# One layer with RWKV-7 and HGRN2 branches: the whole body in one block ordered by a timeline simulation

## The chip, the cores and the metric

The kernel runs on one core of a Trainium2 chip. Its engines are TensorE (PE, matmuls and transposes), VectorE (DVE), ScalarE (ACT), GpSimdE (POOL) and SyncE (SP, which issues DMAs here). Each engine has its own queue of instructions, and the queues meet only at semaphores. The metric is the time of one execution on the device in microseconds (us), the median of several runs; a profile shows one execution.

## The reference, cut to what matters

One layer is applied to a prompt of 512 tokens and to 8 sequences of 4 new tokens each, with their own states. Everything is float32.

```
h   = rmsnorm(x) * norm_mix_g
u   = h @ w_in                       # [tokens, 1024] @ [1024, 5888]
u_a, u_b, u_g = split(u)             # 2048 | 1792 | 2048 columns
o_a = hgrn2(u_a)                     # 4 heads of 128: gated linear attention, norm, gate
o_b = rwkv7(mix(u_b, previous u_b))  # 8 heads of 64: delta rule, group norm, bonus, gate
x   = x + (sigmoid(u_ga) * (o_a @ w_a_out) + sigmoid(u_gb) * (o_b @ w_b_out)) @ w_out
x   = x + square(relu(rmsnorm(x) @ w_up)) @ w_down      # 1024 -> 4096 -> 1024
y   = rmsnorm(x) * norm_final_g
```

Results are y, the last row of h, and the final states of both branches.

## The kernel before

Channels lie on the partitions, and the 512 + 32 tokens (with 8 rows of the shift state for u_b) are the columns, in two halves of about 272, each with a PSUM bank. A float32 weight tile is split into a high part (whi, a copy by ACT to a shorter mantissa) and a low part (wlo, the rest, by DVE), and so are the activations; a product is three groups of matmuls: high by high, low by high, high by low (`split`, line 166, `gemm_h`, line 398).

The program is written as one long Python function, `hybrid_step` (line 61). After the norm of the input (`stats`, `transposed`, `normed`, in the order of the string STARTUP) a loop goes through the string ORDER. Each entry multiplies one column tile of w_in (`in_unit`, line 410: 48 matmuls of 128 x 128 by 128 x 272 or so) and takes it to its place: `b_unit` for RWKV inputs, `a_unit` for HGRN2 inputs, `gate_unit` for the gates. There are 46 such tiles. Between them two background lanes are advanced by a fixed number of steps (`pump`, line 1270); each is a list of Python generators, and a `yield` ends a step.

- Lane X runs `rw_all(0)`, `rw_all(1)` (line 977) and then `hg_head` 3. An `rw_all` prepares two head pairs (`rw_batch`), inverts and solves small triangular blocks (`rw_inverse`, `rw_solve`), carries the state through eight chunks (`rw_chain`, line 760) and normalises the output of each pair (`gn` and `rw_out`, lines 819 and 834). In a step of `rw_chain` each operation needs the one before: pq from the state (PE), ch (DVE), pq from ch (PE), VU (DVE), pq from VU (PE), the state st (DVE). `gn` is a sum, a subtraction, a square (ACT), a sum, an inverse root in twelve small operations (`rsq`, line 143) and a product; `rw_out` transposes (rw_out_pt), scales (og, ACT), adds, gates, and writes og to ob_d in DRAM.
- Lane Y runs `hg_head` 0 and 1, the sample states (`rw_state`, `rw_sample`, `hg_sample`) and `hg_head` 2. `hg_head` (line 1068) scans the decays (hb), goes through five levels and two more in which DVE writes E, ACT takes its exponential, DVE writes X and PE multiplies (hg_head_pl, hg_head_pu; `decayed`, line 1056), masks and adds the products (sm, ad), transposes, makes the state (hst) and the output (hg_head_po, hy), normalises it (squares jk on ACT, `rsq` on DVE) and writes hog to oa_d in DRAM. In PSUM, lane X has two pools of its own and lane Y another.

When ORDER is done the rest of lane X is emitted, then the branch results are read back and merged: `branch(ob_d)` loads ox and splits it into oh (ACT) and ol (DVE); `half_unit` (line 1343) multiplies them by w_b_out, while lane Y is finished; `branch(oa_d)` and w_a_out follow, then `full_unit` (line 1400) for w_out, w_up and w_down. At the end `finish` (line 1455) transposes each channel tile of the result to tokens (fin_t, one PSUM bank), adds up squares and multiplies by the weight; `final` scales and stores.

What sets the order: the framework turns the Python calls into instructions, assigns each to the engine that the call names, and adds the semaphores. A scheduler of its own then puts each engine's instructions in an order; the program gives it the order of the calls and no block of its own. Instructions marked with `tc.keep_in_program_order` (the constants written by POOL, class Late) stay in the order of the calls.

Of the kernel before, what the change touches and what calls it, by code (L numbers as in the profile page):

```python
# [60 lines left out]
def hybrid_step(ctx: ExitStack, tc: tile.TileContext, i, o):  # L61
    nc = tc.nc
# [46 lines left out]
    class Lane:  # L109
        """slots and PSUM banks of one of the two background lanes"""  # L110
# [32 lines left out]
    def rsq(x, scale=None, eps=None):  # L143
        """x <- (x * scale + eps) ** -0.5 of a few columns: a guess from the exponent, three Newton steps"""
        n, m = x.shape
# [28 lines left out]
    def load8(src, c):  # L174
        """columns c..c+128 of a [1024, *] weight as [p, 8, 128]"""
        st = pipe.tile([128, 1024], F32, tag="stage", name=nm("st"), bufs=NST)
        nc.sync.dma_start(out=st.rearrange("p (k c) -> p k c", k=8),
                          in_=src[:, c:c + 128].rearrange("(k p) c -> p k c", p=128))
        return st

# [31 lines left out]
    def stats(t):  # L212
        """1 / rms of every token of a tile, on every partition"""
# [52 lines left out]
    class Late:  # L266
        """Pool operations that stay behind those already queued"""
# [17 lines left out]
    def consts1():  # L285
# [5 lines left out]
        # masks of the RWKV pair products, rows s, columns t: [A_vk^T | A_re^T] over [A_zb^T (negated) | A_rb^T]  # L291
# [8 lines left out]
    def consts2():  # L300
        # masks of the HGRN2 levels inside 32-token blocks: s in the even half, t in the odd half
        late.memset(lmk, 1.0)
        for l, h in enumerate((16, 8, 4, 2, 1)):
            nb = 32 // (2 * h)
            for b in range(4):
                v = lmk[32 * b:32 * b + 32, l, :].rearrange("p (n w) -> p n w", n=nb)
                # t odd half
                late.memset(v[:, :, 0:h], 0.0)
                # s >= 2h*n  and  s < 2h*n + h
# [9 lines left out]
    def consts3():  # L319
        # sample masks: same sequence, strictly causal towards kk, causal towards r  # L320
# [9 lines left out]
        # rows of a sequence: bmk[row, b]  # L330
# [20 lines left out]
    # per-channel parameters, channel on the partition  # L351
# [19 lines left out]
    # sigmoid(x) = (1 + tanh(x / 2)) / 2: halves of the biases, and of the weight behind silu(g)  # L371
# [7 lines left out]
    def load4(src, c):  # L379
        """columns c..c+256 of a [512, *] weight as [p, 4, 256]"""  # L380
# [5 lines left out]
    def gemm(ps, w_hi, w_lo, x_hi, x_lo, n, first=True, last=True, late=0):  # L386
        """lists of [128,128] weight tiles and matching [128, 2n] operands, of which the last few may come late"""
# [10 lines left out]
    def gemm_h(w_hi, w_lo, x_hi, x_lo, cuts, name):  # L398
        """the same products, one bank for each part of the columns"""
# [17 lines left out]
    def b_unit(jt):  # L417
        """column tile jt of the B block -> token-shift mixed [128, 544]"""
# [15 lines left out]
    # low-rank weights: the parts of decay as [hi; lo], of a as [lo; hi], of the gate in two tiles  # L434
# [104 lines left out]
    def head_sums(hi, lo):  # L539
        """sums over the channels of a head, on all of them"""  # L540
# [6 lines left out]
    def rw_batch(pairs, xk, xr, xv):  # L547
        """channel-major preparation and the pair products of two head pairs"""
# [15 lines left out]
        for q, p in enumerate(pairs):  # L564
# [33 lines left out]
            # sample columns: sig, kk, kk*a, k, r, v, bonus  # L598
# [4 lines left out]
            # rows (v side | u side, token), columns (kk | r, token)  # L603
# [22 lines left out]
    def swapped(src, dst):  # L626
        """64x64 transposes within the two halves of the partitions: channels of a head <-> tokens of a chunk"""
# [5 lines left out]
    def rw_values(g):  # L633
        """rows (v | u, token): v, and room for u"""
# [11 lines left out]
    def rw_tokens(p):  # L646
        """A_vk v with rows (head, token); k and b with rows (v | u, token)"""
# [20 lines left out]
    def rw_inverse(g):  # L668
        """(I + A_zb^T)^-1 of the 32x32 diagonal blocks of two pairs.
        16x16 blocks by doubling, one block on a partition (quarter parity, head, half, chunk)"""  # L670
# [39 lines left out]
        # the 32x32 blocks: eight rows of a block on a partition  # L710
# [49 lines left out]
    def rw_chain(g):  # L760
        """the state from chunk to chunk, and the outputs"""
# [850 lines left out]
```

## Time and profile before

| | us |
|---|---|
| median of 3 runs | 1000.02 (999.65 to 1000.9) |
| span of the profiled execution, first to last instruction | 996.1 |
| PE busy | 962.8 |
| DVE busy | 584.3 |
| ACT busy | 394.0 |
| POOL busy | 135.8 |

The profiled execution has no time of its own beside its span; the span lies 3.9 us under the median. A view by stretch gives each engine's busy time between two times, the mean granted clock of PE (1.00 is 2.4 GHz, 0.50 is 1.2 GHz) and the load of the DMA engines. A view in order of time lists an engine's instructions, neighbours that are alike joined in one row with their count; in brackets stands the idle time ahead of a row and what ended it. An instruction's own duration includes its start and its end, and neighbours on one engine overlap by a part of it. Many small matmuls count twice in the trace (8868 there, 7653 in the program).

### The profile page before, as it was taken

How to read it: one execution, taken by the hardware profiler on the slowest of the kernel's cores; microseconds unless marked ns; L12 is line 12 of the kernel's file. 1: busy time of each engine (PE TensorE's matmuls, PEld its weight loads, DVE VectorE, ACT ScalarE, POOL GpSimd, SP SyncE). 2: the span in 40 equal slices, each digit the busy share in tenths (PEclk: the TensorE clock that was granted, in tenths of full speed). 3: DMA queues.
4: the chain of work that ended last, by engine and by line, in shares of the span. 5: the costliest groups of instructions: out<-in, count | busy, mean ns of one | idle time of the engine just before them, and what ended most of it. 6: DMA issues, size and time to landing. Idle time of an engine off the chain costs nothing.

```text
span 996.1 us, 21327 instructions
## 1 busy us (share of the span) xinstructions
PE 962.8 (97%) x8868; PEld 908.1 (91%) x8868; DVE 584.3 (59%) x1198; ACT 394.0 (40%) x722; POOL 135.8 (14%) x328
## 2 busy tenths in 40 slices
PE   5999999999999899999999999999999999999996
PEld 4999988889998886888899999999999999999995
DVE  6635979578696854679878554444222244445333
ACT  7554545514636441334444333333111233333232
POOL 4486423221132101101000000000000000000000
PEclk9999999999999899999999999999999999999998
DMA  9632343222345232445743642322223332234111
GB/s 273 173 105 81 81 91 100 57 66 90 114 107 109 44 107 63 124 135 171 256 122 128 197 128 84 87 85 86 85 86 89 97 90 86 86 106 142 50 44 48
DMA packets 191091, 106.38 MB, mean 107 GB/s; under 512 B 38945, under 2 KB 179047, under 8 KB 190994
## 3 DMA queue, kind: packets, MB, share of 16 engines
q1 hardware_dynamic: 165424, 95.16, 32.8%
q10 hardware_dynamic: 25570, 9.85, 3.9%
q8 instruction: 70, 1.15, 0.5%
q14 instruction: 27, 0.22, 0.1%
HBM read 85.08 MB, written 18.39 MB: 104 GB/s over the span
## 4 chain that ended last, share of the span: by engine, by line
PE 81%; DVE 9%; DMA 4%; ACT 3%; POOL 2%; issue 1%; SPq 1%; ACTq 0%; DVEq 0%; POOLq 0%
PE pd L129 24%; PE in_unit_ps L129 20%; PE full_unit_ps L129 19%; PE half_unit_ps L129 4%; PE rw_chain_pq L129 2%; DVE tmp L135 2%; PE rw_chain_py L129 1%; DVE wlo L135 1%; PE rw_out_pt L129 1%; PE rw_sample_pn L129 1%; PE hg_head_po L129 1%; PE lora_ps L129 1%; DVE bn L724 1%; DMA xin<-in_x_prompt_dram 1%; PE hg_head_pl L129 1%
## 5 line engine op out<-in xcount | busy, mean ns | idle before, releaser
L132 ACT ACTIVATE whi<-st 128x1024 fp32r<-128x1024 f32 x120 | 126.7, 1057 | 251.6 <-PE pd L129 119.2
L135 DVE TENSOR_TENSOR wlo<-st,whi 128x1024 fp32r<-128x1024 f32 x120 | 149.2, 1244 | 126.0 <-PE full_unit_ps L129 40.3
L129 PE MATMUL in_unit_ps<-h_hi,whi 128*128 128x272 f32 (+3 forms) x736 | 121.3, 300 | 2.3 <-ACT h_hi L132 1.4
L129 PE MATMUL in_unit_ps<-h_hi,wlo 128*128 128x272 f32 (+3 forms) x736 | 121.7, 299 | 0.0
L129 PE MATMUL in_unit_ps<-h_lo,whi 128*128 128x272 f32 (+3 forms) x736 | 121.2, 300 | 0.0
L129 PEld LDWEIGHTS in_unit_ps<-h_hi,whi 128*128 128x128 f32 x736 | 103.3, 194 | 8.4 <-issue 3.4
L129 PE MATMUL full_unit_ps<-hd,whi 128*128 128x272 f32 (+2 forms) x832 | 110.3, 289 | 0.0
L129 PEld LDWEIGHTS in_unit_ps<-h_hi,wlo 128*128 128x128 f32 x736 | 103.2, 193 | 4.4 <-issue 2.4
L129 PEld LDWEIGHTS in_unit_ps<-h_lo,whi 128*128 128x128 f32 x736 | 103.7, 194 | 3.8 <-issue 1.9
L129 PEld LDWEIGHTS full_unit_ps<-hd,whi 128*128 128x128 f32 x832 | 106.5, 188 | 0.0
L129 PE MATMUL pd<-xgl,whi 128*128 128x272 f32 x512 | 70.2, 289 | 0.0
L129 PE MATMUL pd<-xgh,wlo 128*128 128x272 f32 x512 | 69.8, 288 | 0.0
L129 PE MATMUL pd<-xgh,whi 128*128 128x272 f32 x512 | 69.8, 288 | 0.0
L141 POOL TENSOR_SCALAR ys<-ys,ssf 32x512 f32<-32x512 f32 x1 | 0.8, 830 | 491.1 <-DVE ssf L1495 491.1
L129 PEld LDWEIGHTS pd<-xgl,whi 128*128 128x128 f32 x512 | 66.7, 188 | 0.0
L129 PEld LDWEIGHTS pd<-xgh,whi 128*128 128x128 f32 x512 | 66.2, 188 | 0.0
L129 PEld LDWEIGHTS pd<-xgh,wlo 128*128 128x128 f32 x512 | 66.2, 188 | 0.0
L129 PE MATMUL full_unit_ps<-hd,wlo 128*128 128x272 f32 (+2 forms) x416 | 56.8, 288 | 0.0
L129 PEld LDWEIGHTS full_unit_ps<-hd,wlo 128*128 128x128 f32 x416 | 54.0, 188 | 0.0
L135 DVE TENSOR_TENSOR hd<-r,hd 128x544 fp32r<-128x544 f32 x32 | 23.2, 725 | 47.9 <-ACT hd L132 47.9
L135 DVE TENSOR_TENSOR x<-x,full_unit_ps 128x272 f32<-128x272 f32 (+2 forms) x48 | 19.5, 434 | 36.9 <-PE full_unit_ps L129 36.9
L138 DVE SCALAR_TENSOR_TENSOR r<-pd,rsb 128x272 f32<-128x272 f32 x64 | 25.2, 435 | 25.9 <-PE pd L129 23.9
(413 smaller groups left out, 1500.9 us busy)
## 6 DMA issues: line engine op xcount, KB each, us to landing
st<-in_w_in_dram SPq DMA_DIRECT2D x46, 512.0 KB
st<-in_w_up_dram SPq DMA_DIRECT2D x32, 512.0 KB
st<-in_w_down_dram SPq DMA_DIRECT2D x32, 512.0 KB
gt_d<-gt SPq DMA_DIRECT2D x16, 272.0 KB
st<-in_w_out_dram SPq DMA_DIRECT2D x8, 512.0 KB
gtb<-gt_d SPq DMA_DIRECT2D x8, 272.0 KB
gta<-gt_d SPq DMA_DIRECT2D x8, 272.0 KB
x<-xt_d SPq DMA_DIRECT2D x8, 272.0 KB
```

What stands on the lines that cost most here:

```text
L129: T.matmul(out, lhsT, rhs, start=start, stop=stop)
L132: A.activation(out=out, in_=in_, func=func, **kw)
L135: (eng or V).tensor_tensor(out=out, in0=a, in1=b, op=op)
L138: V.scalar_tensor_tensor(out=out, in0=a, scalar=s, in1=b, op0=op0, op1=op1)
L141: (eng or V).tensor_scalar(out=out, in0=a, scalar1=s1, scalar2=s2, op0=op0, op1=op1)
L724: V.tensor_reduce(out=o_[:, i0:i1, t0:t1], in_=tp, axis=AX.X, op=ALU.add)
```

## The change

One line is added at the head of `hybrid_step`; the rest of the diff removes comments and docstrings. The line opens a block that lasts to the end of the function, with the option that its instructions are ordered by the scheduler's timeline simulation.

```diff
@@ -59,6 +59,7 @@
 
 @with_exitstack
 def hybrid_step(ctx: ExitStack, tc: tile.TileContext, i, o):
+    ctx.enter_context(tc.block(schedule_with_timeline_sim=True))
     nc = tc.nc
     V, A, P, T = nc.vector, nc.scalar, nc.gpsimd, nc.tensor
     DQ = nc.scalar
@@ -107,7 +108,7 @@
         return psy.tile([128, 512], F32, tag="y", name=nm(name))
 
     class Lane:
-        """slots and PSUM banks of one of the two background lanes"""
+
 
         def __init__(self, S, two, one):
...
         (eng or V).tensor_scalar(out=out, in0=a, scalar1=s1, scalar2=s2, op0=op0, op1=op1)
 
     def rsq(x, scale=None, eps=None):
-        """x <- (x * scale + eps) ** -0.5 of a few columns: a guess from the exponent, three Newton steps"""
+
         n, m = x.shape
         y, t = (small.tile([128, 16], F32, tag=f"rs{e}", name=nm("rs"))[0:n, 0:m] for e in range(2))
         if scale is not None:
...
```

The instructions are the same ones on PE (7653), DVE (1197), POOL (333) and SP (287); ACT has 746 instead of 744, two more loads of its function table. Their order differs on all five engines. In the order after every number behind a tile's name is one higher and every line one further down.

PE, at the place where the products of w_in end and those of w_b_out begin, before (h_hi and h_lo are the normed input; rows that lie between are left out):

```order
L129 MATMUL in_unit_ps_6210<-h_hi,wlo_6207 128x272 x8
L129 MATMUL in_unit_ps_6210<-h_lo,whi_6206 128x272 x8
...
L1159 MATMUL hg_head_pt_5821<-ident,hy_5791 128x128 x4
L1254 MATMUL hg_sample_pt_6017<-ident,hs_5360 128x128
...
L129 MATMUL in_unit_ps_6270<-h_hi,wlo_6267 128x272 x8
...
L129 MATMUL in_unit_ps_6295<-h_hi,wlo_6267 128x272 x8
L129 MATMUL in_unit_ps_6295<-h_lo,whi_6266 128x272 x8
L129 MATMUL hg_head_pl_6326<-X_6331 32x32 x8
L129 MATMUL hg_head_pl_6327<-X_6331 32x32 x8
...
L129 MATMUL half_unit_ps_6423<-oh_6393,whi_6417 128x272
L129 MATMUL half_unit_ps_6436<-oh_6393,whi_6417 128x272
```

The same place after:

```order
L130 MATMUL in_unit_ps_6296<-h_lo,whi_6267 128x272 x8
L130 MATMUL hg_sample_pn_5765<-svm_5763,xt_5540 128x512
L130 MATMUL rw_chain_pq_4894<-st_4708,kr_3680 64x64 x2
...
L130 MATMUL rw_chain_pq_5006<-st_4708,kr_3680 64x64 x2
...
L811 MATMUL rw_chain_pw_5034<-ident,st_4708 64x128
...
L632 MATMUL rw_out_pt_5063<-ident,yo_5030 64x64
...
L130 MATMUL hg_head_pl_5316<-X_5320 32x32 x16
...
L130 MATMUL hg_head_po_5770<-vt_5671,att_5317 128x128 x2
...
L1160 MATMUL hg_head_pt_5822<-ident,hy_5792 128x128 x4
L1255 MATMUL hg_sample_pt_6018<-ident,hs_5361 128x128
L130 MATMUL hg_head_pl_6327<-X_6332 32x32 x8
...
L130 MATMUL half_unit_ps_6424<-oh_6394,whi_6418 128x272
```

Between the last in_unit_ps and the first half_unit_ps stood 33 matmuls, all of hg_head_pl of head 2; now there are 324: three steps of the second chain, its rw_out, head 3 from hg_head_pl to hg_head_pt, the end of hg_sample and the first levels of head 2.

ACT at the same place, before (oa_d<-hog and oa_d<-hs are stores that ACT's queue issues):

```order
L1162 DMA oa_d<-hog_5826 128x512
L132 ACTIVATE gt_6260<-in_unit_ps_6235 128x272
L1258 DMA oa_d<-hs_5361 512x1x32
L132 ACTIVATE E_6376<-E_6376 128x512
L132 ACTIVATE whi_6676<-st_6674 128x1024
L132 ACTIVATE gt_6320<-in_unit_ps_6270 128x272
L132 ACTIVATE E_6468<-E_6468 128x512
L132 ACTIVATE E_6491<-E_6491 128x512
L132 ACTIVATE gt_6320<-in_unit_ps_6295 128x272
L132 ACTIVATE oh_6393<-ox_6391 128x544
```

And after:

```order
L133 ACTIVATE kt_5672<-hg_head_pt_5679 128x512
L133 ACTIVATE hst_5750<-hg_head_pk_5745 128x128
L1142 DMA out_dram<-hst_5750 128x128
L133 ACTIVATE hy_5792<-hg_head_po_5770 128x512
L133 ACTIVATE jk_5794,ss_h<-hy_5792 128x128 x4
L1163 DMA oa_d<-hog_5827 128x512
L1259 DMA oa_d<-hs_5362 512x1x32
L133 ACTIVATE oh_6394<-ox_6392 128x544
L133 ACTIVATE oh_6400<-ox_6398 128x544
```

The first oh now stands behind hy, the squares jk and the two stores; before, exponentials, weight splits and gates of in_units stood between.

PE around the last step of the first RWKV chain (rw_chain_pq_2774 before, rw_chain_pq_2775 after), before:

```order
L129 MATMUL rw_chain_pq_2774<-st_2128,kr_1323 64x64 x2
L129 MATMUL rw_chain_pq_2774<-st_2129,kr_1466 64x64 x2
L129 MATMUL in_unit_ps_3035<-h_lo,whi_3006 128x272 x5
L129 MATMUL in_unit_ps_3171<-h_hi,whi_3167 128x276 x6
L129 MATMUL rw_chain_pq_2774<-ch_2130,TT_1850 64x128
L129 MATMUL rw_chain_pq_2774<-ch_2130,TT_2017 64x128
L129 MATMUL in_unit_ps_3171<-h_hi,whi_3167 128x276 x2
L129 MATMUL in_unit_ps_3171<-h_hi,wlo_3168 128x276 x4
L129 MATMUL rw_chain_pq_2774<-VU_1572,BE_1612 64x64 x2
L129 MATMUL rw_chain_pq_2774<-VU_1572,BE_1652 64x64 x2
L129 MATMUL rw_chain_py_2127<-VU_1572,A_1347 64x64
```

And after, with rows left out:

```order
L130 MATMUL in_unit_ps_4549<-h_lo,whi_4545 128x272 x8
L130 MATMUL rw_chain_pq_2645<-VU_1573,BE_1613 64x64 x2
...
L130 MATMUL rw_chain_pq_2775<-st_2129,kr_1324 64x64 x2
...
L130 MATMUL rw_chain_pq_2775<-ch_2131,TT_1851 64x128
...
L130 MATMUL rw_chain_pq_2775<-VU_1573,BE_1613 64x64 x2
...
L811 MATMUL rw_chain_pw_2825<-ident,st_2129 64x128
...
L632 MATMUL rw_out_pt_2930<-ident,yo_2821 64x64
...
L632 MATMUL rw_out_pt_3095<-ident,yo_2823 64x64
...
L1160 MATMUL hg_head_pt_3495<-ident,hy_3473 128x128 x4
L642 MATMUL rw_batch_pt_4084<-ident,xm_2903 64x128
...
L130 MATMUL in_unit_ps_4574<-h_hi,whi_4545 128x272 x8
```

In_units stood between the parts of the step; now 92 matmuls of the chain's end, of rw_out, of head 1, of the next rw_batch and of rw_state follow each other without one, between two halves of one w_in tile.

## Rows read from the trace of the kernel before

**Rows 1.** The page: busy time of the engines, the chain by engine, one costly group.
```profile
PE 962.8 (97%) x8868; PEld 908.1 (91%) x8868; DVE 584.3 (59%) x1198; ACT 394.0 (40%) x722; POOL 135.8 (14%) x328
...
PE 81%; DVE 9%; DMA 4%; ACT 3%; POOL 2%; issue 1%; SPq 1%; ACTq 0%; DVEq 0%; POOLq 0%
...
L132 ACT ACTIVATE whi<-st 128x1024 fp32r<-128x1024 f32 x120 | 126.7, 1057 | 251.6 <-PE pd L129 119.2
```

**Rows 2.** Busy time by stretch; its columns: stretch, us, engines, PEclk, DMA share, GB/s.
```profile
25.00:485.00 460.00, 449.49 (x4643) 400.58 (x4643) 331.04 (x731) 207.93 (x390) 122.52 (x304) 0.97 0.38 103
485.00:546.00 61.00, 58.78 (x641) 56.07 (x640) 49.18 (x107) 26.01 (x46) 1.53 (x5) 1.00 0.53 171
546.00:985.00 439.00, 439.00 (x3505) 438.68 (x3504) 183.75 (x285) 137.26 (x226) 0.00 (x0) 1.00 0.32 92
```

**Rows 3.** PE in order of time; columns: start us, us, engine, line, operation [idle before].
```profile
484.36 1.17 PE L129 MATMUL in_unit_ps<-h_lo,whi 128*128 128x272 f32 x8
485.45 0.78 PE L129 MATMUL hg_head_pl<-X 128*32 128x32 f32 x66
487.17 0.52 PE L129 MATMUL half_unit_ps<-oh,whi 128*128 128x272 f32 x2 [0.94 <-ACT oh L132]
...
490.42 0.52 PE L129 MATMUL half_unit_ps<-oh,whi 128*128 128x272 f32 x2
```

**Rows 4.** ACT in order of time at the same place.
```profile
486.46 0.66 ACT L132 ACTIVATE oh<-ox 128x544 fp32r<-128x544 f32 x1 [0.51 <-DMA ox<-ob_d]
...
487.98 1.74 ACT L132 ACTIVATE oh<-ox 128x544 fp32r<-128x544 f32 x3
```

**Rows 5.** PE in order of time, one step of the first RWKV chain and the next one's start.
```profile
195.40 0.45 PE L129 MATMUL rw_chain_pq<-st,kr 64*64 64x64 f32 x8
...
199.89 0.45 PE L129 MATMUL rw_chain_pq<-st,kr 64*64 64x64 f32 x8
```

**Rows 6.** DVE in order of time, a norm, its og, an operation of the next one.
```profile
225.21 1.28 DVE L822 TENSOR_REDUCE gs<-yo 128x8 f32<-128x512 f32 x2 [0.65 <-ACT yo L132]
...
235.73 0.68 DVE L135 TENSOR_TENSOR yo<-yo,gs 128x512 f32<-128x512 f32 x1
...
240.93 0.69 DVE L135 TENSOR_TENSOR og<-og,bv 128x512 f32<-128x512 f32 x1 [2.29 <-ACT og L132]
...
246.87 0.17 DVE L135 TENSOR_TENSOR rs<-rs 128x8 f32<-128x8 f32 x1
```

**Rows 7.** PE in order of time, first and last row of a pair's 16 transposes (rows alike between).
```profile
236.59 0.24 PE L631 MATMUL rw_out_pt<-ident,yo 64*64 64x64 f32 x1
...
239.76 0.32 PE L129 MATMUL rw_out_pt<-ident,yo 64*64 64x64 f32 x2
```

**Rows 8.** One window, columns as in Rows 2.
```profile
380.00:500.00 120.00, 118.50 (x1345) 101.10 (x1344) 89.94 (x231) 44.03 (x92) 10.22 (x29) 0.97 0.52 156
```

**Rows 9.** DVE in order of time, two levels of head 2.
```profile
481.82 0.75 DVE L135 TENSOR_TENSOR E<-hb 128x256 f32<-128x256 f32 x2
...
484.17 0.76 DVE L135 TENSOR_TENSOR E<-hb 128x256 f32<-128x256 f32 x2
```

**Rows 10.** DVE in order of time, head 2 from its masked products to its result.
```profile
490.19 0.56 DVE L135 TENSOR_TENSOR sm<-hg_head_pl,lmk 128x384 f32<-128x384 f32 x1 [0.19 <-PE hg_head_pl L129]
...
514.68 0.75 DVE L138 SCALAR_TENSOR_TENSOR hog<-hg_head_pt,prm,xq 128x512 f32<-128x512 f32 x1
```

**Rows 11.** PE in order of time, its longest wait behind 25 us.
```profile
336.83 1.12 PE L129 MATMUL rw_sample_pu<-rs,rs 64*64 64x64 f32 x16 [2.42 <-DVE rs L141]
```

**Rows 12.** Windows behind that wait, columns as in Rows 2.
```profile
337.00:343.00 6.00, 6.00 (x48) 5.51 (x49) 5.08 (x9) 0.43 (x1) 0.00 (x0) 0.50 0.00 0
344.00:345.00 1.00, 1.00 (x19) 0.93 (x20) 0.34 (x1) 0.18 (x1) 0.00 (x0) 1.00 0.28 32
```

**Rows 13.** PE in order of time, the end of the program.
```profile
985.23 0.38 PE L1466 MATMUL fin_t<-ident,x 128*128 128x128 f32 x2
...
986.79 0.44 PE L1466 MATMUL fin_t<-ident,x 128*128 128x128 f32 x2 [0.56 <-DVE yt L135]
```

## The prediction

> **What bounds the kernel now.** I read the page first: TensorE (PE) is busy 97% of the span and the chain that ended last is 81% PE, so whatever moves the end must make PE wait or stop it waiting [rows 1]. Next the busy time by stretch [rows 2]. From 546 to 985 us PE never waits: that is the output projection and the MLP, and its order is left as it was. From 485 to 546 it waits 2 us. Only from 25 to 485 us is there something to win: 460 - 449.5 = 10.5 us of idle, and a granted clock of 0.97 on average, at most 460 x 0.03 = 14 us; together 24 us. What keeps PE full there is the mixture: 2200 large matmuls of in_unit, which depend on little but a split weight tile, stand between the small matmuls of two long serial recipes (the RWKV lane and the HGRN2 lane), each of which waits for VectorE (DVE) or ScalarE (ACT) at every step. Then the join [rows 3]: the last in_unit matmul ends at 485.5, the first half_unit follows at 487.17 and PE is full again from 490.4. The wait there goes back to ACT's oh, the split of the RWKV result that came over DRAM [rows 4].
>
> **The change.** No operation goes or comes but two reloads of ACT's table; all five queues get another order, and each engine works its queue off in that order. So the question is which waits the in_units still cover.
>
> *Behind the last in_unit.* In the order after, 324 small matmuls stand on PE between the last in_unit and the first half_unit, where before there were 33: steps 5 to 7 of the second RWKV chain, its two rw_out, HGRN2 head 3 from its first level to its end, the end of hg_sample, and the first levels of head 2. Before, all but the last stood among in_units. On DVE 160 instructions stand between step 5 of the chain and the first ol, and ACT's first oh stands behind head 3's last squares and behind the two stores of oa_d. PE needs oh, so the half_units wait for the whole of it, though the RWKV result is ready long before. The walk, from the last in_unit matmul to dense half_units:
> (a) three chain steps at 4.5 us, the pace in which a step follows another (195.40 to 199.89) [rows 5]: 13.5; 14 products of hg_sample share DVE and PE, so I take 18 (13.5 to 22).
> (b) The norms of two pairs. From the first sum to the scaled result takes 236.4 - 225.2 = 11.2, then the transposes and ACT's og 4.3 until 240.9 [rows 6, 7]; the second pair's squares are queued behind that og, 23 small operations of 0.17 and four of about 0.7 [rows 6], some 6.7. Together 22 (18 to 26); five levels of head 2 stand in the same stretch, and 60 instructions at 0.39 [rows 8] are 23 us of DVE, so they hide nothing and are hidden.
> (c) Head 3's scan and first levels stand behind the norms in DVE's order: five levels at 484.17 - 481.82 = 2.35 us [rows 9] and some 2 us for the scan and og: 14.
> (d) From the masked products to hog: head 2 took 514.7 - 490.2 = 24.5 us for it before [rows 10], with other work between; head 3 has DVE almost to itself: 22.5 (19 to 24.5).
> (e) Two stores and four oh, as before from 486.5 to 490.4 [rows 3, 4]: 4.
> Sum 80.5 us. Its bounds: 160 instructions at 89.9 / 231 = 0.39 us [rows 8] are 62 us; neighbours overlap by a sixth or so (an estimate: the two E of a level take 0.75 together [rows 9]), so without any wait some 52, plus the 4 of (e): 56. The upper ends together: 91. I take 80, since nearly every step of it is one serial recipe at a time.
>
> *Ahead of the last in_unit.* The 324 matmuls that now lie behind are gone from here: three steps of about 2 us on PE, two pairs' transposes of 3.5 each [rows 5, 7], and some 4 for the rest, 17 us (15 to 20). With in_units earlier PE should also lose fewer waits; of the 24 us that idle and clock can give I take 14 (0 to 24), because the serial recipes still have to be passed and have fewer in_units left to cover them.
>
> *A new gap in the middle.* Between the two halves of one w_in tile (in_unit_ps_4549 and in_unit_ps_4574 in the order after) 92 small matmuls now stand with no in_unit among them: the end of the first chain with its whole last step, both rw_out of its pairs and the start of the next batch. Before, the longest such run outside rw_sample was 40. The walk: one step 4.5, ACT's copies and first norm 9 to 12, transposes and og 4.3, the second pair 6.7 and its transposes 3.5: 27 us, of which PE works some 10. Take 17 us of new idle (12 to 21).
>
> *The clock after a gap.* Before, PE stood 2.4 us until 336.8 [rows 11]; from 337 to 343 the granted clock was 0.50, the 1.2 GHz level, and at 344 it was 1.00 again [rows 12]. That is 6 us at half speed and a part of the two beside them, some 3.3 us lost. I charge it once behind the middle gap and once behind the tail. The Trainium skill, "TensorE: Matmul & The Clock Gate", section "What's actually happening", says that throttled is the default state and that activity releases it; the row agrees. By that rule the sparse matmuls inside the tail too run at 1.2 GHz; that is rival 2.
>
> *Both ends.* At the start ACT splits two weight tiles ahead of the first normed columns, 1.06 us each [rows 1], part of it in time that PE waits anyway: +1.5 (-1 to +3). At the end four fin_t follow the last full_unit where there were two; one round through ACT and DVE takes 986.79 - 985.23 = 1.56 us [rows 13], so +3.1.
>
> **How the numbers follow.** Last in_unit: 485.5 - 17 - 14 + 17 + 3.3 + 1.5 = 476. Dense half_units: 476 + 80 + 3.3 = 559.5 instead of 490.4: +69. With the end +72. The profiled execution spans 996.1 and the median of the runs is 1000.0, so some 4 us lie around the span and stay. 1000 + 72 = **1072 us**.
>
> **Rivals.**
> 1. *The tail is only DVE's work, and the front gives all.* Nothing waits but for DVE's queue: 56 instead of 80, the middle gap 12, the 24 us of the front in full: 485.5 - 17 - 24 + 12 + 3 + 56 + 3 = 518.5, +28, +3 at the end: 1031. For it: DVE is 75% busy from 380 to 500 [rows 8], so it holds work to fill with. Against: levels and norms are strictly one behind the other in the new order.
> 2. *PE at 1.2 GHz through the whole tail.* The PE steps on the tail's path (three steps of some 1.5, three groups of matmuls of 0.45 or more in each, 7 of transposes, some 4 of head 3) double [rows 12]: +12, 1084. For it: PE would be idle most of the tail, and the clock fell before after 2.4 us of idle. Against: the steps of [rows 5, 7] are as much latency as columns.
> 3. *More places where a queue's head blocks.* The new order also puts wlo and evacuations of in_unit banks behind instructions that wait (ACT's xk of one in_unit stands behind the copies and squares of the norms in the middle gap). One more gap like that one, 20 us with its clock, and the tail at its upper end: 1102.
> 4. *Faster.* The gain of the front, at most 24 us and the 17 us of work taken out, wins if the tail is shorter than what it gives: the last in_unit could end at 485.5 - 41 = 444.5, and dense work starts earlier than 490.4 if the tail takes under 46 us. Then, with the tail hidden down to 30 us, say, 1000 - 16 + 3 = 987. Against: 160 DVE instructions alone need 52, and the first of them waits for matmuls behind the last in_unit.
> 5. *The order does little*, within 0.2%. Against it stands the order itself: matmuls that hid among in_units have none left.
>
> Chances: the forecast 0.43, rival 1 0.14, rival 2 0.22, rival 3 0.14, faster 0.04, nothing 0.03. Slower by over 0.2% 0.93 (0.2%, 2 us, is about what a measurement of this kernel can tell from no change). The range goes from rival 1 to just short of rival 3, 1030 to 1100: it leaves out half of rival 3, and rivals 4 and 5.
>
> **What would show it.** In the profile after: the last in_unit matmul near 476 (450 to 490); a stretch of 70 to 90 us behind it in which PE is busy less than a third; ACT's first oh at its end, released by head 3 and not by the DMA of ox; a second hole of about 17 us early on, at the second half of one w_in tile, from the first chain's last step to its rw_out; the granted clock at 0.5 behind both; four fin_t at the end; and from the first dense half_unit to the last full_unit the same 495 us as before. It is wrong if oh comes while head 3 still runs, if the tail takes under 56 us, or if PE idles above 5 us in further places.

## The result and the profile after

The kernel after takes **1115.6 us** (median of 4 runs, 1112.8 to 1116.8) against 999.8 us before in the same comparison: ratio 1.116, interval 1.113 to 1.119. Slower, as forecast, but by 115 us and not by 72, and outside the range given (1030 to 1100). The profiled execution spans 1111.0 us against 996.1, so 114.9 us are to be accounted for.

The page of after, its busy times, the granted clock in 40 slices and the chain by engine [rows 1]:

```profile
PE 978.8 (88%) x8868; PEld 922.4 (83%) x8868; DVE 586.3 (53%) x1198; ACT 398.3 (36%) x724; POOL 134.2 (12%) x328
...
PEclk9999989899956799995558899999999999999998
...
PE 74%; DVE 13%; ACT 4%; DMA 4%; issue 3%; POOL 1%; SPq 0%; ACTq 0%; DVEq 0%; POOLq 0%
```

Every engine does the work it did. PE is busy 978.8 us instead of 962.8 (16.0 more for the same matmuls, and two stretches lie near the 1.2 GHz level) and idle 132.2 instead of 33.3 (98.9 more); together 114.9. In the clock row, where before has 8 or 9 in every slice, two dips to 5 stand: the hole in the middle and the tail. By stretch (stretch, us, then the busy us of PE, PEld, DVE, ACT and POOL, PEclk, DMA share, GB/s), as [rows 2]; PEld is the loading of weights:

```profile
25.00:298.90 273.90, 262.08 (x2641) 247.62 (x2640) 167.57 (x323) 123.70 (x224) 89.83 (x238) 0.98 0.34 94
298.90:371.10 72.20, 31.12 (x194) 23.81 (x194) 43.17 (x104) 32.21 (x46) 15.75 (x24) 0.61 0.19 53
371.10:497.80 126.70, 124.16 (x1367) 110.60 (x1367) 69.89 (x156) 40.17 (x87) 12.97 (x33) 0.98 0.39 104
497.80:592.90 95.10, 49.00 (x657) 33.62 (x657) 59.77 (x170) 21.10 (x45) 4.33 (x13) 0.56 0.28 85
```

The last in_unit ends at 497.8 (485.5 before), half_units are dense from 592.9 (490.4). Of the 114.9 us, 12.3 are there at the last in_unit, 90.2 more are added by the tail (95.1 against 4.9), 9.6 between dense half_units and the last full_unit, 2.9 at the end.

**The same, read along the RWKV lane.** The ledger above says where PE stood, not why. The lane that the half_units wait for is one serial recipe, so I cut the time at its stations: the first and last rw_chain_pq<-st,kr of either chain, and the first half_unit. The two chains, from the view of this tile on PE (xcount: duration min/median/max ns, first to last start us), before and then after:

```profile
L129 PE MATMUL rw_chain_pq<-st,kr x56: 218/218/267, 190.2 to 219.9; 64*64 64x64 f32 x56
L129 PE MATMUL rw_chain_pq<-st,kr x56: 216/218/267, 365.2 to 401.1; 64*64 64x64 f32 x56
```
```profile
L130 PE MATMUL rw_chain_pq<-st,kr x56: 218/218/267, 228.3 to 298.1; 64*64 64x64 f32 x56
L130 PE MATMUL rw_chain_pq<-st,kr x56: 218/218/366, 452.4 to 512.1; 64*64 64x64 f32 x56
```

| station, us | before | after | difference |
|---|---|---|---|
| first chain starts | 190.2 | 228.3 | +38.1 |
| first chain | 29.7 | 69.8 | +40.1 |
| to the second chain | 145.3 | 154.3 | +9.0 |
| second chain | 35.9 | 59.7 | +23.8 |
| to the first half_unit (487.2, 589.6) | 86.1 | 77.5 | -8.6 |

The sum is 102.4, the delay of the first half_unit. So the lane's way through the tail isn't what got longer: from the chain's end to the first half_unit it takes less time than before. It is 111 us late when it gets there, and the in_units that covered it are used up. Busy time in these stretches, after and then before:

```profile
228.30:298.10 69.80, 69.80 (x663) 63.96 (x662) 27.12 (x58) 18.83 (x41) 7.78 (x24) 1.00 0.27 80
298.10:452.40 154.30, 110.05 (x1125) 95.37 (x1120) 93.64 (x211) 61.24 (x107) 24.63 (x43) 0.80 0.29 75
452.40:512.10 59.70, 56.90 (x551) 46.31 (x550) 27.37 (x66) 12.48 (x27) 5.54 (x19) 0.92 0.50 144
512.10:589.60 77.50, 34.24 (x507) 23.87 (x503) 49.14 (x147) 18.14 (x41) 3.12 (x9) 0.54 0.19 57
```
```profile
190.20:219.90 29.70, 29.70 (x350) 23.77 (x351) 20.45 (x58) 5.56 (x16) 6.95 (x17) 1.00 0.10 30
401.10:487.20 86.10, 85.13 (x929) 75.44 (x925) 69.95 (x186) 35.51 (x79) 5.71 (x16) 0.96 0.53 158
```

The first row of after is the one to look at. PE is busy 69.80 of 69.80 us at full clock: by PE's idle time this is the best stretch of the program. But DVE is busy 39% there, where it was 69% before. The lane isn't held by its own operations; it is queued on PE behind filler.

**One link.** One step of the first chain in after, in order of time (start us, us, engine, line, operation):

```profile
264.74 0.45 PE L130 MATMUL rw_chain_pq<-st,kr 64*64 64x64 f32 x8
...
265.12 1.03 PE L130 MATMUL in_unit_ps<-h_lo,whi 128*128 128x272 f32 x6
265.24 0.61 DVE L139 SCALAR_TENSOR_TENSOR ch<-rw_chain_pq,av 64x128 f32<-64x128 f32 x2 [1.77 <-PE rw_chain_pq L130]
...
265.98 1.16 PE L130 MATMUL in_unit_ps<-h_hi,whi 128*128 128x272 f32 x8
...
266.98 1.17 PE L130 MATMUL in_unit_ps<-h_hi,wlo 128*128 128x272 f32 x8
...
267.99 0.41 PE L130 MATMUL in_unit_ps<-h_lo,whi 128*128 128x272 f32 x2
...
268.33 0.65 PE L130 MATMUL rw_chain_pq<-ch,TT 128*64 128x128 f32 x4
...
273.57 0.48 DVE L139 SCALAR_TENSOR_TENSOR st<-rw_chain_pq,pcs,ch 128x64 f32<-128x64 f32 x2 [3.64 <-PE rw_chain_pq L130]
...
276.74 0.45 PE L130 MATMUL rw_chain_pq<-st,kr 64*64 64x64 f32 x8
```

DVE has ch ready at 265.85; PE takes it up at 268.33, behind 24 in_unit matmuls. The state st is ready at 274.05; PE takes it up at 276.74. The step lasts 12.0 us and holds 73 in_units. In [rows 5] it lasted 4.49, and the first of its links in between read:

```profile
195.78 0.91 PE L129 MATMUL in_unit_ps<-h_lo,whi 128*128 128x276 f32 x5
195.89 0.59 DVE L138 SCALAR_TENSOR_TENSOR ch<-rw_chain_pq,av 64x128 f32<-64x128 f32 x2 [1.19 <-PE rw_chain_pq L129]
...
196.52 0.29 PE L129 MATMUL in_unit_ps<-h_hi,whi 128*128 128x276 f32 x1
...
196.74 0.65 PE L129 MATMUL rw_chain_pq<-ch,TT 128*64 128x128 f32 x4
```

Six in_units there, just as long as DVE needs for ch; 13 in the step. Counted in the orders of PE's queue, of the 2208 in_units:

| in_units that stand | before | after |
|---|---|---|
| ahead of the first chain's links | 972 | 1155 |
| in the first chain's links | 96 | 405 |
| between the chains | 643 | 387 |
| in the second chain's links | 96 | 261 |
| behind the second chain | 401 | 0 |

Eight in_units take 1.00 us (265.98 to 266.98). So 309 more in the first chain are 38.6 us of delay (40.1 measured), 165 more in the second 20.6 (23.8 measured, of which 146 of the 165 lie between the stations), 183 more ahead of the first 22.9 of the 38.1. Another 5.2 of the 38.1 are more idle time of PE (11.2 us from 25 to 228.3, 6.0 from 25 to 190.2 before); the last 10 are other matmuls.

**The hole and the tail.** The largest waits of PE in the hole and behind the last in_unit (start us, us, operation, in brackets the wait and its releaser), with what DVE and ACT did in the middle:

```profile
308.93 0.28 PE L632 MATMUL rw_out_pt<-ident,yo 64*64 64x64 f32 x1 [7.09 <-DVE yo L136]
...
348.87 2.18 PE L130 MATMUL in_unit_ps<-h_hi,whi 128*128 128x272 f32 x8 [10.17 <-ACT xk L133]
...
371.14 1.27 PE L130 MATMUL in_unit_ps<-h_hi,whi 128*128 128x272 f32 x4 [9.39 <-DVE xq L139]
```
```profile
341.69 3.53 DVE L567 RECIPROCAL nrm<-nrm 128x544 f32<-128x544 f32 x1
...
347.68 0.71 DVE L139 SCALAR_TENSOR_TENSOR al<-al,xm 128x544 f32<-128x544 f32 x1
```
```profile
348.42 0.69 ACT L133 ACTIVATE xk<-in_unit_ps 128x272 f32<-128x272 f32 x2 [4.35 <-DVE al L139]
```
```profile
534.39 0.28 PE L632 MATMUL rw_out_pt<-ident,yo 64*64 64x64 f32 x1 [12.37 <-DVE yo L136]
...
545.52 0.28 PE L632 MATMUL rw_out_pt<-ident,yo 64*64 64x64 f32 x1 [5.97 <-DVE yo L136]
...
583.18 1.12 PE L1160 MATMUL hg_head_pt<-ident,hy 128*128 128x128 f32 x4 [5.10 <-DVE hy L136]
...
589.64 0.52 PE L130 MATMUL half_unit_ps<-oh,whi 128*128 128x272 f32 x2 [2.42 <-ACT oh L133]
...
629.60 1.27 PE L130 MATMUL half_unit_ps<-oh,whi 128*128 128x272 f32 x4 [6.39 <-ACT oh L133]
```

In the middle not only the norm's yo is waited for. Two in_units wait for the evacuation of their bank into xk and xq; ACT's xk reads nothing of the lane, but waits for DVE's al. The likely reason is its slot: al reads an xm, and xm and xk come from the same pool (of NS_O slots). And al stands behind the recipe of the second batch, with its two RECIPROCALs of 3.5 us on DVE and, from 326 to 371 us, nine loads of ACT's function table of 1.28 us each. So filler is there, and is locked behind the lane.

### The profile page after: what moved, and what is told of

Read it like the earlier page. It is cut to its first block, busy times and chain, and to the rows that moved or that the text cites. A ratio compares the mean times of both kernels' runs of the same rounds, so it can differ in the third digit from the quotient of the medians.

```text
span 1111.0 us, 21366 instructions
## 1 busy us (share of the span) xinstructions
PE 978.8 (88%) x8868; PEld 922.4 (83%) x8868; DVE 586.3 (53%) x1198; ACT 398.3 (36%) x724; POOL 134.2 (12%) x328
## 4 chain that ended last, share of the span: by engine, by line
PE 74%; DVE 13%; ACT 4%; DMA 4%; issue 3%; POOL 1%; SPq 0%; ACTq 0%; DVEq 0%; POOLq 0%
PE pd L130 21%; PE in_unit_ps L130 20%; PE full_unit_ps L130 17%; PE half_unit_ps L130 4%; PE rw_chain_pq L130 2%; PE rw_out_pt L130 1%; ACT L133 1%; PE rw_chain_py L130 1%; DVE E L136 1%; DVE tmp L136 1%; DVE X L136 1%; PE rw_out_pt L632 1%; PE lora_ps L130 1%; PE hg_head_po L130 1%; DVE wlo L136 1%
## 5 line engine op out<-in xcount | busy, mean ns | idle before, releaser
L130 PE MATMUL in_unit_ps<-h_hi,wlo 128*128 128x272 f32 (+3 forms) x736 | 117.2, 298 | 0.0
L130 PE MATMUL in_unit_ps<-h_lo,whi 128*128 128x272 f32 (+3 forms) x736 | 116.8, 294 | 0.0
L130 PEld LDWEIGHTS in_unit_ps<-h_lo,whi 128*128 128x128 f32 x736 | 101.3, 190 | 4.0 <-issue 2.7
L632 PE MATMUL rw_out_pt<-ident,yo 64*64 64x64 f32 x32 | 9.8, 306 | 31.3 <-DVE yo L136 31.3
```

What stands on the lines that cost most here:

```text
L130: T.matmul(out, lhsT, rhs, start=start, stop=stop)
L632: (mm if h else T.transpose)(dst[r, 64 * n:64 * n + 64], src[r, 64 * n:64 * n + 64], ident[r, r])
```

## Experiments

The theories. **Cover** (theory A where in_units are held back, against rival C, the orders of the other engines): only in_units are missing where PE stands; give them back and the time returns. **Links (F)**: the order puts too many in_units into the chain's links, so that the lane comes late and they run out. **Order (G)**: it is the order of the lanes' small operations, on PE or on the engines that feed it. Where whole queues are forced, the expectations call it theory A that PE's order costs the time and theory B that the feeding engines' orders do; D and S are VectorE's and ScalarE's alone, and B is then a share of each.

**Is it the block or the simulation?**

```
-    ctx.enter_context(tc.block(schedule_with_timeline_sim=True))
+    ctx.enter_context(tc.block())
```

> The block is opened at the same place, but without the option that orders it by the timeline simulation; the order on all engines is that of the kernel before. If the order alone makes the difference: 998 to 1002 us, like the kernel before. If a block of its own costs something (another start or end): above 1003.

1000.8 us against 999.4, ratio 1.0015 (0.9987 to 1.0043). The block costs nothing; the order by simulation costs all.

**Are in_units missing where PE stands?** Three kernels keep the simulation but hold each in_unit matmul behind a small matmul that was traced some 200 earlier: for all 46 tiles of w_in, for the first 25, for the last 21.

```
+                    p = old + (new - old) * n // 48 - 200
+                    held = name == "in_unit_ps" and p > 0
+                    with tc.issue_after(lane[p]) if held else ExitStack():
```

> The changed kernel, but each matmul of in_unit has to stand on TensorE behind one of the small matmuls that the program wrote some 200 matmuls earlier, spread evenly over the 48 of a tile; no wait is added, only order, and the other engines are ordered by the simulation around that. Theory A (TensorE ran out of in_units: they were ordered too early, and the serial recipes stood alone in the middle and behind the last one): 990 to 1015 us, TensorE idle below 45 us, no stretch of 50 us with TensorE busy under 60%. Rival C (the new orders of VectorE, ScalarE and SyncE block at their heads by themselves): above 1050, with the waits of TensorE on ScalarE's oh and xk still there.

> As the run before, but only the first 25 of the 46 tiles of w_in are held back; the other 21 come as early as the simulation puts them. Theory A: the hole of 298.9 to 371.1 us goes (41 us of idle and some 10 of low clock), the 324 matmuls alone behind the last in_unit stay: 1055 to 1085 us, the stretch between the last in_unit and dense half_units 85 to 105 us. Rival C: no better than 1100.

> Only the last 21 tiles of w_in are held back. Theory A: the stretch behind the last in_unit shrinks from 95 us to under 15, and those tiles fill the middle as well: 1000 to 1045 us. If the middle hole is its own trouble (buffer slots held by the RWKV inputs): 1030 to 1060, with an idle stretch of over 25 us still near 300 us. Rival C: no better than 1100.

1085.6, 1098.6 and 1090.4 us (ratios 1.087, 1.099, 1.091, each to 0.005), all over what theory A gave. In mix200 96 small matmuls of the 324 were left between the last in_unit and the first half_unit, and still 30 us of 115 are all that came back. In mix200 the wait for yo is 7.3 us instead of 31.3, and new ones took its place, the largest for a reciprocal root of rw_sample:

```profile
PE rw_sample_ps L72 <- DVE rs L151: 10.5, 1, 10.5
```

Its links still held up to 26 in_units, where before had at most 11. Cover alone falls as the reason.

**Whose order?** Here an engine's whole queue is forced into the order that it has before (or after) by a chain of order edges without semaphores; the others are ordered anew around it.

```
+    for places in ORDERS:          # per engine: places in the text, in its order before
+        for p, q in zip(places, places[1:]):
+            tc.add_manual_dep(traced[q], traced[p].name, NoSync)
```

> The changed kernel with TensorE's whole order set to that of the kernel before, matmul by matmul; the simulation orders VectorE, ScalarE, GpSimdE and SyncE around it. Theory A (TensorE's order costs the time): 995 to 1010 us. Theory B (the orders of the engines that feed TensorE bring the serial recipes late, and TensorE's order only follows from it): above 1040, with the idle time of TensorE spread over many waits for VectorE and ScalarE instead of two stretches.

> The changed kernel with the orders of VectorE, ScalarE, GpSimdE and SyncE set to those of the kernel before, and TensorE's left to the simulation. In the order 64 matmuls instead of 324 stand between the last in_unit and the first half_unit. Theory A: above 1040, since TensorE's order is still the simulation's. Theory B: 995 to 1025.

> The other way round: the kernel before in a block ordered without the simulation, with TensorE's order set to that of the changed kernel (324 matmuls behind the last in_unit, 92 in the middle). Theory A: 1095 to 1125 us, both stretches as in the changed kernel. Theory B: below 1095; at least the 92 and the 324 matmuls find their inputs earlier, so both stretches are shorter than 72 and 95 us.

> The kernel after with the whole order of TensorE and of VectorE forced to that of before; ScalarE, GpSimd and SyncE stand as the simulation puts them for it. pe_as_before, with TensorE's order alone, took 1070.8. Theory D (the 70 us that stay there are VectorE's order: small operations of one recipe put in between another's): 1000 to 1015. Theory S (ScalarE's order, evacuations and splits behind norms that wait): 1050 to 1075. Theory B (each a share): 1020 to 1050.

> The kernel after with the whole order of TensorE and of ScalarE forced to that of before; VectorE, GpSimd and SyncE stand as the simulation puts them. Theory D (VectorE's order holds the rest): 1050 to 1070. Theory S (ScalarE's): 1000 to 1015. Theory B (each a share, or the two only together): 1020 to 1050.

> The kernel after with the whole orders of TensorE, VectorE and ScalarE forced to those of before; GpSimd and SyncE by the simulation. If the shares add (TensorE's order alone takes after from 1115.6 to 1070.8, VectorE's with it to 1030.6, ScalarE's with TensorE's to 1054.3: 40 and 16 of 71), some 15 us stay for the two that are left: 1012 to 1018. If the last step needs VectorE and ScalarE together (each waits for the other), 998 to 1006, and GpSimd's and SyncE's order costs nothing.

| order of before forced on | us | ratio to before, interval |
|---|---|---|
| none (after) | 1115.6 | 1.116, 1.113 to 1.119 |
| PE | 1070.8 | 1.072, 1.069 to 1.076 |
| DVE, ACT, POOL, SP | 1081.1 | 1.083, 1.076 to 1.089 |
| PE, ACT | 1054.3 | 1.055, 1.052 to 1.058 |
| PE, DVE | 1030.6 | 1.030, 1.025 to 1.035 |
| PE, DVE, ACT | 1008.1 | 1.006, 1.003 to 1.008 |
| no simulation, PE in the order after | 1130.8 | 1.133, 1.129 to 1.136 |

PE's order after is enough by itself to cost 133 us when the default scheduler orders the rest around it, and with PE alone left to the simulation 83 us stay. So neither theory A nor theory B holds alone. Each run against the kernel before of its own comparison: PE's order of before returns 43 of 116, VectorE's with it 41 more, ScalarE's with both 24. What is left, 7, is GpSimd's and SyncE's by subtraction; no run forces these two alone. The shares depend on what was taken back before: ScalarE's is 18 behind PE's alone and 24 behind PE's and VectorE's. What one such wait looks like, pe_as_before shows. First a wait on PE, then DVE's rows ahead of it:

```profile
317.27 1.12 PE L1160 MATMUL hg_head_pt<-ident,hy 128*128 128x128 f32 x4 [12.21 <-DVE hy L136]
```
```profile
304.74 3.56 DVE L567 RECIPROCAL nrm<-nrm 128x544 f32<-128x544 f32 x1
...
310.46 3.55 DVE L567 RECIPROCAL nrm<-nrm 128x544 f32<-128x544 f32 x1
...
314.50 0.15 DVE L139 SCALAR_TENSOR_TENSOR ss_h<-rs,rs 128x4 f32<-128x4 f32 x1
...
316.53 0.68 DVE L136 TENSOR_TENSOR hy<-hy,ss_h 128x512 f32<-128x512 f32 x1
```

The Newton steps for hy, at most 0.17 us each, are put in between the operations of RWKV's next batch, two of 3.5 us among them, and PE stands for 12.2 us. The Trainium skill, "TensorE: Matmul & The Clock Gate", has in the table under its title that VectorE's queue is strictly first in, first out; these rows agree, since hy's small steps don't pass the RECIPROCAL.

**The slots.** If xk waits because its slot is held, more slots should free it. Two more in the pool of xm and xk (and two less in another, for room):

```
-NS_X = 28
-NS_O = 12
+NS_X = 26
+NS_O = 14
```

> The changed kernel with 14 slots instead of 12 for the results of in_unit, and 26 instead of 28 for the recipes of the RWKV lane. If the middle hole stands where the slots run out (xk of a tile waits until the RWKV inputs are read): the hole stands one or two tiles of w_in later (its 128 matmuls without an in_unit now begin behind tile 34 instead of 33), the in_units that ran early are missing at the end, where 428 instead of 324 matmuls stand alone: 1110 to 1150 us. If the hole is only the serial recipes' own length and slots don't matter: the same place and 1110 to 1120.

1102.0 us: 13.6 less than after, and under both expectations. The wait for xk is gone, one of 11.9 us for xq stays. The simulation gives another order for other slots (the chain starts at 252.9 instead of 228.3), so this doesn't price the slot by itself; it only shows that two more slots don't bring the time back.

**The number of in_units in the links.** In a plain block, PE's queue is forced into an order in which in_units stand at other places among the small matmuls. First the numbers of after in both chains, spread evenly, in the order of before (where 265 small matmuls had to move too); and the reverse, numbers near those of before in the order after.

```
-PE: 972, 96 in chain 1, 643, 96 in chain 2, 401      (before)
+PE: 972, 405, 570, 261, 0                            links_stuffed
-PE: 1155, 405, 387, 261, 0                           (after)
+PE: 1155, 110, 600, 100, 243                         links_capped
```

> The kernel before in a plain block, with TensorE's small matmuls in the order of before, but its in_unit matmuls stand elsewhere among them, in the numbers of the order after: between the first and the last link of the first chain of rw_chain 405 in_unit matmuls instead of 96, in the second chain 261 instead of 96, between the two chains 570, and behind the second chain none where before had 401 (the first 972 stay). The other engines get the order that the default scheduler gives them for this. Theory F (the links of the chain are over-filled: in_units that later steps need as cover are used up while the lane could go on; nothing else is wrong with the simulated order): the 401 in_units, 401 x 0.12 = 48 us of TensorE's work, are no longer there for the norms of the second chain and HGRN2's head 3, so TensorE stands behind them for 45 to 70 us and at 1.2 GHz; 1045 to 1090, with PE idle up by 40 or more. Theory G (where the in_units stand makes no matter as long as the small matmuls keep their order; the loss is in that order): within 1000 to 1020.

> The kernel of pe_as_after (1130.8 us) with one thing different: TensorE's small matmuls stand in the order after, but in_unit matmuls are taken out of the chain's links and stand later: 110 instead of 405 in the first chain, 600 instead of 387 between the chains, 100 instead of 261 in the second, 243 instead of none behind it, each spread evenly. Theory F (over-filled links): the hole in the middle and most of the tail close, at least 60 of the 130 us come back: 1030 to 1070. Theory G (the order of the small matmuls is what costs): 1100 or more, with waits on the lanes in many places instead of two.

1276.6 and 1478.3 us: far over every expectation, so both tell nothing of the number. The two have in common that in_units stand one by one between small matmuls. The control keeps the five numbers of before and sets them one by one:

```
-PE: in_units of a zone in 150 clumps
+PE: the same number in each zone, in 802 places
```

> The kernel before in a plain block, with as many in_unit matmuls in each of the five zones as before (972, 96, 643, 96, 401), but set one by one, evenly between the small matmuls of the zone: 802 places with in_units instead of 150. It tells whether links_stuffed and links_capped (1276.6 and 1478.3, far over both theories) were slow because of the numbers or because of the single setting. If the setting is what cost there: 1150 to 1350, with a granted clock near 0.6 from 220 us to the last in_unit though the profile counts PE as busy. If the numbers did: within 995 to 1020.

1410 to 1469 us: the setting alone costs over 400. A window and three rows of PE:

```profile
600.00:960.00 360.00, 347.86 (x1415) 218.88 (x1413) 92.17 (x233) 44.70 (x93) 10.17 (x31) 0.51 0.17 50
```
```profile
641.03 0.69 PE L130 MATMUL rw_chain_pq<-ch,TT 128*64 128x128 f32 x2
641.64 0.60 PE L130 MATMUL in_unit_ps<-h_hi,whi 128*128 128x272 f32 x1
642.17 0.69 PE L130 MATMUL rw_chain_pq<-ch,TT 128*64 128x128 f32 x2
```

PE counts as 97% busy there, at a granted clock of 0.51; an in_unit takes 0.53 from its start to the next row's, where eight in a row took 0.125 each in after. links_capped has the same picture:

```profile
500.00:900.00 400.00, 376.46 (x1495) 235.16 (x1494) 99.71 (x230) 46.81 (x97) 9.51 (x28) 0.55 0.13 38
```

So the next kernels make clumps longer or shorter instead, and first in the second chain alone. In the 165 dose every small matmul stands as before; in the 401 dose 50 had to move.

```
-PE: 972, 96, 643, 96, 401      (before)
+PE: 972, 96, 643, 261, 236     second_chain_165
+PE: 972, 96, 643, 497, 0       second_chain_401
```

> The kernel before in a plain block, with one thing changed on TensorE: in the second chain of rw_chain 261 in_unit matmuls (the number of the order after) stand between its links instead of 96, in the same clumps made longer (links_stuffed had set them one by one, also inside a link's group, and so told nothing of the number). The 165 are taken from the 401 that stood behind that chain; every small matmul stands as before. The other engines get the default scheduler's order. Theory F (over-filled links): the chain ends some 165 x 0.12 = 20 us later with 236 in_units left as cover for what comes behind it, which needs its old time; the end moves by 10 to 25 us: 1010 to 1025. Theory G (the number in the links makes no matter): 998 to 1004.

> As second_chain_165, but all 401 in_units that stood behind the second chain now stand between its links (497 in it), none behind it, as in the order after. Theory F: the chain ends some 48 us later and TensorE stands alone with the lanes behind it, at 1.2 GHz: 48 us and some 6 of clock less what waits the front saves, 1040 to 1060, with PE idle up by 30 or more, all of it behind the last in_unit. Theory G: 998 to 1010.

1017.0 us (ratio 1.016, 1.013 to 1.019) and 1048.3 us (1.046, 1.043 to 1.050): +16 and +47, inside what F gave in both doses, 0.10 and 0.12 us for each in_unit moved. The second dose, its second chain and what follows:

```profile
367.70:444.80 77.10, 76.91 (x688) 65.75 (x687) 28.34 (x63) 19.39 (x39) 5.42 (x18) 1.00 0.38 112
444.80:527.60 82.80, 45.97 (x534) 32.33 (x529) 56.69 (x153) 19.81 (x44) 6.39 (x11) 0.60 0.35 105
```

That is the picture of after in small: a chain of 77.1 us instead of 35.9 in which PE is full, then the tail, 82.8 us (86.1 before) with PE 46 us busy at a clock of 0.60. Its in_units ran out 10.6 us after the chain's last station. And the reverse, in clumps, in the order after:

```
-PE: 1155, 405, 387, 261, 0         (pe_as_after)
+PE: 1155, 200, 500, 100, 253       clumps_capped
```

> The kernel of pe_as_after (1130.8 us) with every small matmul where it was, but with the in_units moved as links_capped was meant to: 200 instead of 405 in the first chain's links, 500 instead of 387 between the chains, 100 instead of 261 in the second chain's, 253 instead of none behind it, in clumps at places where the order before or after has one (links_capped had them one by one). Theory F (over-filled links are most of the loss): 50 to 90 us come back, 1040 to 1080. Theory G (the order of the small matmuls costs): 1100 or more.

1109.9 us against 1130.8 of pe_as_after (ratios 1.109 and 1.133): 21 us back, in the bound that G gave, where F wanted 50 to 90. The chains got shorter (47.4 and 47.1 us), but the first starts at 240.0 and PE waits for the lanes elsewhere, most of all here:

```profile
PE rw_out_pt L632 <- DVE yo L136: 18.6, 3, 7.4
```

So the links are a cause with a price of its own, shown in two doses; they aren't the whole. Once the small operations stand in the order after, taking most of the added in_units out of the links returns a sixth. What in that order holds the other 109 us isn't settled beyond the shares of the engines above: no run takes the order of PE's small matmuls apart further.

## Why the prediction was right and wrong

- *Direction, and the two holes*: right in mechanism. The hole in the middle lies at the second half of one w_in tile, the tail behind the last in_unit, the clock is 0.61 and 0.56 in them, and no gain of the order outweighed them.
- *Ahead of the last in_unit*: **the step that failed**. It took 17 us out for matmuls that moved behind and 14 as a gain from waits and clock, and put in one hole of 17 with 3.3 of clock and 1.5 at the start: the last in_unit at 476. It came at 497.8; -9.5 forecast, +12.3 measured. From 25 us to the last in_unit PE idled 10.5 us before [rows 2]; after, it idled 41.1 in the hole and 14.4 beside it (11.8 and 2.5). So the hole was 24 us too small, and of the gain from waits nothing came; some 4 us were lost instead. An error the other way hid 16 us: PE's busy time there fell by 33 (450.0 to 417.4), not by 17. What the step left at nothing is the time that the lane stands on PE behind the in_units of its own links. The pace of [rows 5] belongs to the 13 in_units that stood in that step. The order on which the prediction rests already said 405 and 261 instead of 96 and 96, and at 0.125 us each that is 59 us of delay for the lane. That such a delay costs time by itself is shown by the two doses (16 and 47 us); how much of the miss here is its, no run tells.
- *The hole in the middle*, in that step: 17 us of idle forecast, 41.1 measured (72.20 - 31.12), and PE's work in it at a clock of 0.61. The terms of the walk add up to 28 to 31 us, not to 27. What it counted, from the last chain step to the second pair's og, came out: 27.1 us with 13.6 of idle.

```profile
298.90:326.00 27.10, 13.51 (x82) 8.79 (x82) 12.47 (x52) 4.07 (x8) 0.21 (x1) 0.59 0.17 51
```

  Not counted were the 45 us behind it with the other 27.5 of idle: the second batch's recipe, and the in_units that stand behind it in the queue, whose evacuation it locks (10.2 and 9.4 us of wait). That was in rival 3, which named ACT's xk behind other recipes and gave one more gap of 20 us; it was the rival to weigh more.
- *The tail*: 80 us and 3.3 of clock forecast, 95.1 measured from the last in_unit to dense half_units. (a) chain steps 18, measured 20.9 (497.8 to 518.7). (b) norms 22, measured 31.8: sums begin 3.2 us after the chain, the first norm takes 12.3 instead of 11.2, and the 16 transposes of the second pair, which the step left out, 5.2. (c) levels 14, measured 12.3. (d) 22.5, measured 22.3. (e) 4, measured 7.8; the first oh is released by the landing of the second store, at 588.93. So one term was short by 10 us and two by 3 and 4. That the clock stays low through the whole tail (rival 2) is right: 0.56, and a pair's transposes take 5.2 us instead of 3.5. The Trainium skill, "TensorE: Matmul & The Clock Gate", section "What's actually happening", says that throttled is the default state and that activity releases it; the 0.56 over 95.1 us with PE busy half the time agrees.
- *Half_units to the last full_unit*: 0 forecast, +9.6. The half_units wait 6.4 us for oh at 629.60. This oh needs head 2's result, whose store is issued at 623.96, 31 us after half_units became dense; before, hog was done 25 us after that [rows 3, 10], and PE waited for no oh there.
- *The end*: +3.1 forecast, +2.9 measured, with the four fin_t as said [rows 13]:

```profile
1097.28 0.38 PE L1467 MATMUL fin_t<-ident,x 128*128 128x128 f32 x2
...
1102.06 0.44 PE L1467 MATMUL fin_t<-ident,x 128*128 128x128 f32 x2 [0.89 <-DVE yt L136]
```

- *The signs*: two of the named ones failed. PE was busy 49.0 of the tail's 95.1 us, half and not under a third. And it idles above 5 us in further places, which the prediction called a sign that it is wrong: 10.2 and 9.4 us in the hole, 6.4 at 629.60.

Together: 21.8 us missed ahead of the last in_unit (the hole is in it), 11.6 in the tail, 9.6 behind it, -0.2 at the end: 42.8 of the 42.7 between 72.2 and 114.9. The time lies 115 us up and not 72, and over rival 3's 1102 as well.

## What to carry to other kernels

Where large matmuls cover a serial recipe, count how many stand in each of its links: enough for the other engine's answer, and no more, for a stretch in which PE is 100% busy can be one that makes the program late. Look at the feeding engine's share there (DVE 39% instead of 69%) and at the stations of the serial path, not at PE's idle time, which shows up only where the cover has run out. And when an order is changed, price each engine's queue: taken back one after the other, three of them returned 43, 41 and 24 us of the loss here.

## What the runs showed of the hardware

In_units set one by one between small matmuls ran at a granted clock of 0.51 over 360 us in clumps_to_singles, though the profile counted PE as 97% busy there, and at 0.55 over 400 us in links_capped, with PE 94% busy. The same number in clumps ran at 0.97 in the kernel before, from 25 to 485 us [rows 2]. So a busy share near 1 doesn't say that PE is at 2.4 GHz; the clock column has to be read beside it. Whether the clock or the lost overlap of neighbours came first there, no run tells.
